# The mixer of a hybrid encoder gets a block and an instruction planner of its own

## The chip, the core and the metric

The kernel runs on one core of one Trainium2 chip. The core has five engines that each work through their own list of instructions in order: TensorE (PE, with its weight loads shown apart as PEld), VectorE (DVE), ScalarE (ACT), GpSimd (POOL) and SyncE (SP), which here issues all DMA transfers. They wait for one another through semaphores. The metric is the device time of one execution in microseconds (us).

## The reference

One layer of an encoder for 2048 tokens of width 1024, in float32. A mixer first, whose input projection feeds two recurrences: an mLSTM with 4 heads of 128, chunked, and an RWKV-7 recurrence with 8 heads of 64, in which each token changes a 64 x 64 state per head. Then attention to a memory of 256 tokens, then a gated feed-forward net with a causal convolution, each with a residual and an RMS norm:

```python
x = x + hybrid_token_mixer(rmsnorm(x, norm_mix), ...)       # mLSTM and RWKV-7 side by side
x = x + mem_cross_attn(rmsnorm(x, norm_x), rmsnorm(mem, norm_mem), x_wq, x_wkv, x_wo)
x = x + conv_glu_ffn(rmsnorm(x, norm_ffn), f_up, f_conv_w, f_conv_b, f_down)
return rmsnorm(x, norm_final)
```

and inside the mixer, for the RWKV-7 half, token by token:

```python
sk = einsum('bhvk,bhk->bhv', state, kk_t)
state = state * w_t - sk[..., None] * (kk_t * a_t) + v_t[..., None] * k_t
y = einsum('bhvk,bhk->bhv', state, r_t)
```

## The kernel before

Matrix products of weights and activations are done in two parts: a weight tile of 512 KB is loaded (`load_raw`, line 96), rounded by ScalarE into `whi` (line 101), and the rest is taken by GpSimd or VectorE into `wlo` (line 105); three products hi x hi, hi x lo, lo x hi follow. Two raw tiles and four split pairs are kept.

The first part, `mixer()`, goes over four blocks of 512 tokens. `norm_block` makes the normalised block `hA` (eight tiles, hi and lo); the dense products `pd<-hA` (31 weight tiles for each block, line 122 by the helper `mm`) feed seven streams. `rwkv_pre` prepares a head pair (16 groups in all: 4 blocks by 4 pairs), `rwkv_solve` inverts the small triangular matrices on VectorE with several round trips through DRAM, `rwkv_merge` puts them together, and `rwkv_seq` runs the recurrence over 8 chunks of each group, 128 steps in all. One step is a chain over three engines: PE makes `qy` from the state `sbd`, ACT copies `q`, PE makes `pu`, DVE copies it to `UV` (line 755), PE makes `pS` from `UV`, DVE updates `sbd` (line 761). `rwkv_tail` normalises the result. `st_ml` does the mLSTM in the same manner, and `gates` makes the gates of each block (with the transposes `gtr`). At the end of `mixer()`, `kv_prep` folds the keys and values of the memory with the query and output weights into `qk_dram` and `vo_dram`; its 32 weight tiles use the same two raw tiles, and its `mem` tiles the eight slots of `hA`.

The function `run_streams` sets the program order of all this: it calls the streams' generators one piece at a time, on a clock that counts estimated PE time alone, with waits such as `yield LU` (178 ns between `pu` and `pS`) or `LSOLVE` (39163 ns from a group's `rwkv_pre` to its merge).

Program order is not yet the engines' order. The framework plans each block of a program before it is compiled: it steps through a simulated execution, and each engine takes, among the instructions whose inputs and buffers are ready at that simulated moment, the one that stands first in program order. That fixes every engine's list, SyncE's DMA issues among them. Which instructions count as ready hangs on the durations that the planner assumes. There are two planners: the ordinary one, and one that uses a full timeline simulation of engines and queues. A block opened with `tc.block` is planned by itself, and no instruction of it is mixed with those outside. In the kernel before, the constants at the top and the whole of `mixer()` stand in the program's outer block and are planned by the ordinary one; the second part (output projection, attention, feed-forward) has been opened as

```python
ctx.enter_context(tc.block(name="attn_ffn", schedule_with_timeline_sim=True))
```

Of the kernel before, what the change touches and what calls it, by code (L numbers as in the profile page):

```python
# [56 lines left out]
def tile_hybrid_encoder(ctx: ExitStack, tc: tile.TileContext, t_in: dict, out: bass.AP, stage: str = "all"):  # L57
# [1055 lines left out]
        kv_prep(kt, sm, T, PQ, PD)  # L1113
        mx.close()

    mixer()
    wld[0] = 0
    if stage == "mix":
        nc.sync.dma_start(out, y_dram.rearrange("k p t -> (k p) t"))
# [361 lines left out]
```

## Time and profile before

| | us |
|---|---|
| median of 3 runs | 3570.65 |
| lowest and highest | 3564.45, 3571.49 |
| the profiled execution's own time | 3564.44 |
| its span, first to last instruction | 3562.6 |
| mixer, by the windows of the trace | 0 to 1515 |
| second part | 1515 to 3562 |

The profiled execution is one of the quicker ones: 6.2 us under the median. A busy time is the time in which an engine works on an instruction; a wait row says for which instruction of which engine an idle engine waited.

### The profile page before, as it was taken

To read this page: it belongs to the slowest core of one execution; us is meant where nothing else is said; L and a number is where in the kernel's file an instruction comes from. 1 tells how busy PE (TensorE), PEld (TensorE's weight loads), DVE (VectorE), ACT (ScalarE), POOL (GpSimd) and SP (SyncE) were. 2 spreads that over 40 slices of the span, in tenths; PEclk is the share of its full clock that TensorE was granted. 3 is DMA by queue.
4 is the path that set the end of the run, shared out by engine and by line. 5 is a ranking of instruction groups with operands and counts; after the bars stand their busy time and mean duration, and the time that the engine had idled before them with its cause. 6 is when DMAs were issued, how large, how long until landed. Compare 5 with 4: busy or idle time off the path is not lost.

```text
span 3562.6 us, 48272 instructions
## 1 busy us (share of the span) xinstructions
PE 3377.6 (95%) x17836; PEld 2750.2 (77%) x17836; DVE 2020.6 (57%) x4038; ACT 1256.2 (35%) x2397; POOL 1368.7 (38%) x1364
## 2 busy tenths in 40 slices
PE   7999999999989999789999999999999999999997
PEld 5777777777767778668888888888788888888886
DVE  6788888878888887433333343444453344344345
ACT  5345434544454444433222212212442222222213
POOL 5233333433333322353144434434632343443433
PEclk9999999999999999899999999999999999999998
DMA  4223222322222234685621111112566411111111
GB/s 131 80 67 111 77 72 75 111 70 68 90 73 69 73 94 146 212 269 177 222 71 43 59 42 54 54 36 71 154 219 212 141 55 36 54 54 42 54 48 54
DMA packets 203388, 342.01 MB, mean 96 GB/s; under 512 B 77072, under 2 KB 108944, under 8 KB 203152
## 3 DMA queue, kind: packets, MB, share of 16 engines
q1 hardware_dynamic: 203152, 338.92, 30.2%
q8 instruction: 141, 2.31, 0.3%
q14 instruction: 95, 0.78, 0.1%
HBM read 293.68 MB, written 45.15 MB: 95 GB/s over the span
## 4 chain that ended last, share of the span: by engine, by line
PE 55%; DMA 4%; DVE 2%; ACT 1%; issue 0%; POOL 0%; SPq 0%; DVEq 0%; ACTq 0%; POOLq 0%
PE pd L148 11%; PE pd L151 11%; PE pd L150 11%; PE dps L1354 4%; PE dps L1352 4%; PE dps L1353 4%; DMA x<-xT 2%; PE sc L1233 1%; PE sc L1235 1%; PE sc L1234 1%; DVE x L1369 0%; DMA wqk<-qk_dram 0%; PE ppt L1258 0%; DVE x L1201 0%; DMA y<-y_dram 0%
## 5 line engine op out<-in xcount | busy, mean ns | idle before, releaser
L105 POOL TENSOR_TENSOR wlo<-wraw,whi 128x512 fp32r<-128x512 f32 (+1 forms) x544 | 785.7, 1451 | 813.0 <-ACT whi L101 736.3
L122 PE MATMUL pd<-hA,whi 128*128 128x512 f32 x1984 | 677.6, 415 | 11.2 <-ACT uconv L824 5.8
L101 ACT CAST whi<-wraw 128x512 fp32r<-128x512 f32 (+1 forms) x596 | 383.4, 651 | 540.9 <-PE pd L150 222.0
L151 PE MATMUL pd<-h,wlo 128*128 128x512 f32 x1408 | 547.9, 389 | 0.0
L148 PE MATMUL pd<-h,whi 128*128 128x512 f32 x1408 | 547.9, 389 | 0.0
L150 PE MATMUL pd<-h,whi 128*128 128x512 f32 x1408 | 547.7, 389 | 0.0
L122 PEld LDWEIGHTS pd<-hA,whi 128*128 128x128 f32 x1984 | 357.5, 191 | 80.4 <-ACT hA L363 8.3
L122 PE MATMUL pd<-hA,wlo 128*128 128x512 f32 x992 | 402.2, 405 | 0.0
L1355 DVE TENSOR_TENSOR x<-dps,x 128x512 f32<-128x512 f32 x352 | 235.5, 689 | 224.3 <-PE dps L1354 222.2
L150 PEld LDWEIGHTS pd<-h,whi 128*128 128x128 f32 x1408 | 264.3, 188 | 54.8
L151 PEld LDWEIGHTS pd<-h,wlo 128*128 128x128 f32 x1408 | 264.3, 188 | 54.8
L148 PEld LDWEIGHTS pd<-h,whi 128*128 128x128 f32 x1408 | 264.3, 188 | 54.7
L1354 PE MATMUL dps<-act,wlo 128*128 128x512 f32 x704 | 271.5, 390 | 0.0
L1353 PE MATMUL dps<-act,whi 128*128 128x512 f32 x704 | 271.4, 390 | 0.0
L1352 PE MATMUL dps<-act,whi 128*128 128x512 f32 x704 | 261.6, 390 | 3.2 <-DVE x L1355 2.6
L122 PEld LDWEIGHTS pd<-hA,wlo 128*128 128x128 f32 x992 | 189.8, 191 | 34.2 <-issue 0.7
L1336 DVE SCALAR_TENSOR_TENSOR fu<-fu,pd 128x512 f32<-128x512 f32 x88 | 60.5, 688 | 226.6 <-PE pd L151 221.7
L1155 POOL TENSOR_TENSOR sq<-sq 128x512 f32<-128x512 f32 x56 | 73.9, 1320 | 252.9 <-ACT sq L1152 231.5
L1352 PEld LDWEIGHTS dps<-act,whi 128*128 128x128 f32 x704 | 132.6, 188 | 31.9 <-DVE x L1355 3.4
L1354 PEld LDWEIGHTS dps<-act,wlo 128*128 128x128 f32 x704 | 132.6, 188 | 27.6
L1353 PEld LDWEIGHTS dps<-act,whi 128*128 128x128 f32 x704 | 132.4, 188 | 27.5
L1330 POOL TENSOR_TENSOR fu<-fu,bcs 128x512 f32<-128x512 f32 x88 | 114.2, 1298 | 97.1 <-DVE fu L1329 95.6
(913 smaller groups left out, 6220.2 us busy)
## 6 DMA issues: line engine op xcount, KB each, us to landing
wraw<-w_in SPq DMA_DIRECT2D x124, 512.0 KB, 3.5
wraw<-f_up SPq DMA_DIRECT2D x88, 512.0 KB, 3.4
wqk<-qk_dram SPq DMA_DIRECT2D x64, 512.0 KB, 5.3
wvo<-vo_dram SPq DMA_DIRECT2D x64, 512.0 KB, 4.2
wraw<-f_down SPq DMA_DIRECT2D x44, 512.0 KB, 3.4
wraw<-w_out SPq DMA_DIRECT2D x32, 512.0 KB, 5.6
y<-y_dram SPq DMA_DIRECT2D x32, 256.0 KB, 7.0
x<-xT SPq DMA_DIRECT2D x32, 256.0 KB, 5.1
```

Source lines behind the costliest of these rows:

```text
L101: nc.scalar.copy(hi, raw)
L105: (nc.vector if dve else nc.gpsimd).tensor_tensor(lo, raw, hi.bitcast(F32), ALU.subtract)
L122: nc.tensor.matmul(out_, lhsT, rhs, **kw)
L148: nc.tensor.matmul(ps, hi[:, k % 4, :], a[:, 0, :n], start=(k == 0), stop=False)
L150: nc.tensor.matmul(ps, hi[:, k % 4, :], a[:, 1, :n], start=False, stop=False)
L151: nc.tensor.matmul(ps, lo[:, k % 4, :], a[:, 0, :n], start=False, stop=(k == last and not late))
L1155: (nc.vector if fast else nc.gpsimd).tensor_tensor(acc, acc, sq, ALU.add)
L1330: nc.gpsimd.tensor_tensor(u, u, bc3[b], ALU.mult)
L1352: nc.tensor.matmul(ps, hi[:, d, :], a[:, 0, :], start=(g == 0), stop=False)
L1353: nc.tensor.matmul(ps, hi[:, d, :], a[:, 1, :], start=False, stop=False)
L1354: nc.tensor.matmul(ps, lo[:, d, :], a[:, 0, :], start=False, stop=(g == GRP - 1))
L1355: nc.vector.tensor_tensor(xs[b][d], ps, xs[b][d], ALU.add)
```

## The change

```diff
@@ -1113,7 +1113,8 @@
         kv_prep(kt, sm, T, PQ, PD)
         mx.close()
 
-    mixer()
+    with tc.block(name="mixer", schedule_with_timeline_sim=True):
+        mixer()
     wld[0] = 0
     if stage == "mix":
         nc.sync.dma_start(out, y_dram.rearrange("k p t -> (k p) t"))
```

The call of `mixer()` is enclosed in a block of its own, which is planned on the full timeline simulation. The few constants made before it (`ident`, `vec`, `ones`, `nhalf`, `align`) stay in the outer block. No instruction of the computation is added, removed or changed in size; program order, tiles and buffers are the same.

## Rows read from the trace of the kernel before

**Rows 1.** Part 1 of the page: the span, then busy time by engine.

```profile
span 3562.6 us, 48272 instructions
PE 3377.6 (95%) x17836; PEld 2750.2 (77%) x17836; DVE 2020.6 (57%) x4038; ACT 1256.2 (35%) x2397; POOL 1368.7 (38%) x1364
```

**Rows 2.** Windows by stage: start:end, length, busy us (instructions) of each engine, granted clock.

```profile
core 0: us, PE busy (x) PEld busy (x) DVE busy (x) ACT busy (x) POOL busy (x), PEclk, DMA share, GB/s
0.00:100.00 100.00, 73.61 (x323) 58.26 (x323) 62.49 (x121) 58.18 (x107) 55.57 (x106) 0.97 0.40 132
100.00:1340.00 1240.00, 1151.29 (x7561) 906.57 (x7561) 1018.60 (x2547) 558.64 (x1180) 418.55 (x482) 0.98 0.27 80
1340.00:1431.00 91.00, 80.21 (x646) 71.18 (x646) 64.29 (x161) 43.15 (x106) 28.35 (x25) 0.92 0.49 152
1431.00:1515.00 84.00, 66.77 (x381) 57.42 (x379) 37.67 (x49) 34.63 (x64) 24.88 (x19) 0.88 0.70 219
1515.00:3562.00 2047.00, 2005.75 (x8928) 1656.74 (x8928) 837.52 (x1164) 561.64 (x940) 841.37 (x732) 0.99 0.30 96
```

**Rows 3.** Waits of PE up to 1515 us: total us, times, longest.

```profile
PE pS L122 <- DVE UV L755: 41.1, 43, 2.7
PE gtr L126 <- ACT xs L515: 15.0, 4, 5.3
PE ssa L322 <- DVE sq L319: 14.4, 1, 14.4
PE qy L122 <- DVE sbd L761: 12.2, 20, 2.0
```

**Rows 4.** Tile hA, the dense products: duration ns min/median/max, first and last start.

```profile
L122 PE MATMUL pd<-hA,wlo x992: 387/393/776, 21.9 to 1318.6; 128*128 128x512 f32 x199
```

**Rows 5.** Tile UV: the copy on VectorE.

```profile
L755 DVE COPY UV<-pu x128: 247/283/285, 183.7 to 1420.1; 64x128 f32<-64x128 f32 x128
```

**Rows 6.** Tile sbd: the state update on VectorE.

```profile
L761 DVE SCALAR_TENSOR_TENSOR sbd<-pS,pcol,sp x256: 240/284/293, 185.2 to 1421.8; 64x64 f32<-64x64 f32 x128
```

**Rows 7.** Tile KR: a product with two operands in SBUF.

```profile
L613 DVE TENSOR_TENSOR KR<-xs,Pt x32: 406/414/1516, 74.8 to 1310.1; 128x256 f32<-128x256 f32 x32
```

**Rows 8.** Line 105, the splits of weights, 0 to 1340 us.

```profile
L105 POOL TENSOR_TENSOR wlo<-wraw,whi x230: 1262/1291/2562, 5.5 to 1317.8; 128x512 fp32r<-128x512 f32 x115
```

**Rows 9.** Timeline around one step of the recurrence: start us, length us.

```profile
1298.91 1.53 POOL L105 TENSOR_TENSOR wlo<-wraw,whi 128x512 fp32r<-128x512 f32 x1 [1.91 <-ACT whi L101]
1299.21 1.51 DVE L613 TENSOR_TENSOR KR<-xs,Pt 128x256 f32<-128x256 f32 x1
1299.38 0.40 PE L122 MATMUL pu<-q,dg 128*66 128x64 f32 x4
...
1300.75 0.28 DVE L755 COPY UV<-pu 64x128 f32<-64x128 f32 x1
...
1301.09 0.49 PE L122 MATMUL pS<-UV,E 128*128 128x128 f32 x2 [0.56 <-DVE UV L755]
```

**Rows 10.** Windows around two waits of PE, columns as in Rows 2.

```profile
255.00:268.00 13.00, 10.34 (x63) 8.02 (x61) 12.02 (x40) 3.35 (x9) 4.29 (x6) 1.00 0.22 65
1018.00:1030.00 12.00, 9.67 (x59) 8.45 (x60) 7.78 (x23) 4.69 (x11) 1.76 (x3) 0.59 0.24 76
```

**Rows 11.** Waits of SyncE's queue up to 1515 us.

```profile
SPq L96 <- POOL wlo L105: 183.0, 34, 14.8
```

**Rows 12.** Timeline at the start of the program.

```profile
0.81 0.39 SPq L70 DMA_DIRECT2D vec<-vec  x1
0.94 0.06 DVE L78 MEMSET align<- 128x1 f32 x1
```

**Rows 13.** Timeline at the present border between mixer and second part.

```profile
1514.92 0.06 DVE L78 MEMSET align<- 128x1 f32 x1
1515.47 0.83 SPq L96 DMA_DIRECT2D wraw<-w_out  x1
...
1522.95 0.79 PE L148 MATMUL pd<-y,whi 128*128 128x512 f32 x1 [9.33 <-ACT y L1184]
```

## Prediction

> **What bounds the kernel now.** I read the page's first part, then windows cut where the work changes, then PE's waits, then the tiles of the recurrence. The span is 3562.6 us and PE is busy for 3377.6 us of it [rows 1]. The windows show two unlike halves [rows 2]. From 1515 us on PE works for 2005.8 of 2047 us at a granted clock of 0.99: the second part, which the change leaves alone. In the mixer PE is busy for 1151 of 1240 us between 100 and 1340 us and VectorE for 1019 of them (82%), so two engines are nearly full there and the lists of both matter. In the last 175 us, to 1515, PE leaves 28 us empty and the clock falls to 0.92 and 0.88.
>
> What PE waits for is a list of short waits, not one long one [rows 3]: 41.1 us in 43 waits for the copy to `UV`, 12.2 us in 20 for the state `sbd`, 15.0 us in four for the gates, and 14.4 us before its first product. A wait for `UV` or `sbd` is one of an order: PE's list has `pS` or `qy` at its head while dense products stand behind it, and the timeline shows one. `pu` starts at 1299.38, the copy at 1300.75 and `pS` at 1301.09, because VectorE was busy with the product of line 613 from 1299.21 on for 1.51 us [rows 9]. The copy itself never takes over 0.285 us and the state update never over 0.293 [rows 5, 6]: what is late is the place in VectorE's list.
>
> **The change, part by part.**
>
> *The new border.* The block ends the free mixing of the constants with the mixer. At the present border PE stands idle for 9.33 us, but that is a reload: the first weight tile is issued at 1515.47, and PE starts at 1522.95 [rows 13]. VectorE's first instruction behind it, a memset of 0.06 us, runs at 1514.92, half a us before that load is issued [rows 13], so the border itself is no long meeting of all engines. At the new one nothing stands before it but the load of `vec`, issued at 0.81 us, and memsets that end by 1 us [rows 12]. Bounds: 0, if engines pass it one by one, and 9.3, the whole hole of the other border. I take 1.5 us, near the lower end, since the mixer's first load can start some 1 us later at most.
>
> *The work.* Nothing is removed, added or resized: the 7561 matmuls and 2547 VectorE instructions of the middle window [rows 2], and every DMA, are issued again. All five lists are drawn up afresh, and SyncE's with them.
>
> *The stalls of the recurrence.* This is the term that decides. There are 128 steps, each with one copy to `UV`. 43 of them hold PE up now, a third, at 41.1/43 = 0.96 us each [rows 3]. Below: a planner whose durations match the chip would see `UV` late and put dense products before `pS`; none is hit, a gain of 41.1 us. Above: with no foresight at all a copy finds VectorE busy in 82% of cases [rows 2], 105 of 128 steps, and 105 x 0.96 = 101 us, a loss of 60 us. Which end is nearer? Whether a step is hit hangs on what VectorE does in that microsecond, and the same instruction there takes 0.41 us mostly and 1.52 at worst [rows 7]: in the timeline, 1.51 us while a GpSimd split of 1.53 us ran beside it [rows 9]. A plan fixes one duration for each instruction and one place for each split; on the chip the lists drift against each other for 1500 us, so a truer mean does not say which step is met. Against that, dense products are there to be put between. I take half of the steps: 64 x 0.96 = 61.4, so 20.3 us more than now. The `sbd` waits, 20 at 0.61 us, I leave where they are; the same scaling would add 52 us at the upper end (105 x 0.61 less 12.2).
>
> [...]
>
> *The tail.* Dense products end at 1318.6 us [rows 4]; the recurrence makes its last state update at 1421.8 [rows 6], and `kv_prep` goes on alone to 1515. The `mem` tiles sit in slots of `hA`, so `kv_prep`'s products can't be pulled before that moment by any plan. If dense work ends earlier the tail starts earlier; if the recurrence falls behind, it sticks out longer, with `kv_prep` to fill it. PE has 28 us empty there [rows 2]; a plan could gain or lose that much, and I take zero.
>
> *The second part* starts from the same DRAM tensors and its own plan: zero, give or take its first 9.3 us.
>
> Sum against the profiled execution: 3564.44 + 1.5 + 20.3 = 3586.2 us. The median shown lies 6.2 us above that execution, so 3592.4 us for a median. A change under 0.2% (7.1 us) can't be told from none in this kernel.
>
> **The rivals.**
>
> *Faster: the stalls go.* In the old planner's own picture PE cannot stand idle before `pS` with a ready dense product behind; on the chip it does so 43 times, so that picture has VectorE too quick. The full timeline may have it right. Then up to 41.1 + 12.2 = 53.3 us go, and with them lowered clock: in the stretch around the longest wait for the gates, 5.3 us, the granted clock is 0.59, though around the longest wait for `UV`, 2.7 us, it is 1.00 [rows 3, 10], so short waits cost little of it. The shortfall from 1.00 over the mixer's windows is 3 + 25 + 7 + 10 = 45 us [rows 2]. Half of the stalls and a quarter of the shortfall: 26.7 + 11.3 - 1.5 = 36.5 us gained, 3534 us. All of both would give 3474. Against it: the UV wait above, which no mean duration foretells. It decides from the point where fewer than 43 steps are hit.
>
> *Much slower: SyncE's queue.* All transfers stand in one list. Its issues of weight loads wait 34 times for a GpSimd split that frees a raw tile, 183 us together, 5.4 us each and 14.8 at most [rows 11]; behind them stand the small transfers of `rwkv_solve`. Today no wait of PE in the mixer is for a DMA among its largest [rows 3]. If the new list puts one such wait in front of each group's round trip and merges stand too early in PE's list, 16 x 5.4 = 86 us are added: 3658 us. For it: the order of program has only an estimate of the solve's length in it. It decides when the merge's first transposes wait for their load.
>
> *No change.* The two planners agree on nearly all of the order, or the block is planned as before, and the border's 1.5 us is all: 3572 us.
>
> **How the numbers follow.** More hits, as summed: 0.45. SyncE's queue: 0.09. No change: 0.10. Faster: 0.36. The first two are slower, 0.54 together. The likeliest case gives 3592 us; its own range runs from 3578, just beyond what can be told, to 3640 (3570.65 + 60 + 9.3), the two upper bounds together. The range given must hold both signs: its low end is 3512, 22 us below the faster case, and its high end 3650, short of the queue's case. I leave about 0.09 on each side.
>
> **What would show it.** Right: PE's wait for `UV` above 60 us in the mixer's window, with the number of waits nearer to 64 than 43, PE's busy time there about the same, and the dense products ending some 20 us later than 1318.6. For the faster rival: that wait well below 41 us, a clock nearer 1.00 to 1340 us, and the second part starting near 1480. For the queue: waits of PE on `dg` loads, and long SyncE waits ahead of the round trips. If all lists stand as before, the trace repeats the old waits one by one. The forecast is wrong if the new planner knows VectorE's delays well enough to fill the steps; and it is wrong in its place, not its sign, if the loss sits in the tail after the last dense product instead of in the steps.

## The result and the profile after

The change makes the kernel slower: 3768.96 us median of four runs (3761.37 to 3773.94) against 3567.55, a ratio of 1.0562 with a 95% interval of [1.054, 1.0585], 201 us. The forecast was 3592.4, at most 3650: the sign is right, the size is not. The profiled execution took 3761.37 us. Two executions marked as slow are left out of all numbers below, one of x18's four at 12290.68 us and one of the kernel before at 3788.9 us.

Part 1 of the page after, to be held against [rows 1]:

```profile
span 3759.6 us, 48403 instructions
PE 3513.0 (93%) x17836; PEld 2904.9 (77%) x17836; DVE 1971.9 (52%) x4038; ACT 1262.7 (34%) x2397; POOL 1367.3 (36%) x1364
```

The same 17836 products keep PE busy for 3513.0 us, 135 us more than before; VectorE's 4038 instructions take 49 us less. Windows by stage (start:end, length, then each engine's busy us and instructions; then the granted clock, the mean share of TensorE's full clock in that window), cut as in [rows 2] at the last dense product, the last state update and the border:

```profile
0.00:100.00 100.00, 79.29 (x367) 64.11 (x368) 67.02 (x131) 61.83 (x113) 56.94 (x110) 1.00 0.41 133
100.00:1470.00 1370.00, 1225.27 (x7057) 1006.55 (x7056) 905.04 (x2341) 533.89 (x1104) 407.17 (x463) 0.85 0.23 69
1470.00:1709.00 239.00, 203.93 (x1484) 179.04 (x1483) 161.73 (x397) 103.83 (x240) 60.12 (x57) 0.84 0.52 157
1709.00:1717.00 8.00, 2.16 (x6) 0.71 (x4) 2.03 (x5) 1.41 (x2) 3.00 (x3) 0.50 0.01 3
1717.00:3759.60 2042.60, 2002.31 (x8928) 1654.53 (x8928) 836.07 (x1166) 561.74 (x940) 840.07 (x733) 0.99 0.30 96
```

The second part is untouched (2042.6 us, clock 0.99); the mixer grows from 1515 to 1717 us. PE's busy time in it is 79.29 + 1225.27 + 203.93 + 2.16 = 1510.7 us, before it was 73.61 + 1151.29 + 80.21 + 66.77 = 1371.9 [rows 2]: 139 us of the 202 are PE working longer on the same products, at a clock of 0.85 in place of 0.98 in the long middle window, and 63 us are PE standing empty. The first 100 us are better than before (PE 79.3 against 73.6).

Where the work ends, from the tiles hA and sbd (duration ns min/median/max, first and last start), against [rows 4, 6]:

```profile
L122 PE MATMUL pd<-hA,wlo x992: 387/389/628, 24.3 to 1469.4; 128*128 128x512 f32 x199
L761 DVE SCALAR_TENSOR_TENSOR sbd<-pS,pcol,sp x256: 243/290/324, 193.7 to 1707.4; 64x64 f32<-64x64 f32 x128
```

The last dense product comes 151 us later, the last state update 286. The recurrence trailed the dense products by 103 us at the end; now it trails by 238, and ends together with `kv_prep`. PE's waits in the mixer (total us, times, longest), against [rows 3]:

```profile
PE pS L122 <- DVE UV L755: 42.4, 35, 7.0
PE qy L122 <- DVE sbd L761: 29.6, 11, 7.3
PE ssa L322 <- DVE sq L319: 14.7, 1, 14.7
PE qy L122 <- ACT yt L768: 12.7, 17, 2.1
```

The wait that the forecast built on, `UV`, has hardly moved in sum (41.1 before) and strikes fewer steps, 35 for 43. The other direction has moved. VectorE's waits before the change, mixer:

```profile
DVE UV L755 <- PE pu L122: 35.2, 36, 2.3
...
DVE sbd L761 <- PE pS L122: 16.3, 24, 1.2
```

and after it:

```profile
DVE UV L755 <- PE pu L122: 100.4, 60, 9.0
DVE sbd L761 <- PE pS L122: 74.3, 66, 4.4
DVE pr L676 <- DMA l<-rd: 57.9, 15, 7.0
```

Now VectorE stands with the recurrence's instruction at its head and waits for PE's products, 174.7 us in place of 51.5. PE is late with the recurrence. In VectorE's longest wait for `pu`, 9.0 us, PE works through 35 dense products (start:end, length, PE busy us on them, their number, granted clock):

```profile
984.80:993.80 9.00, 8.04 (x35) 1.00 0.31 110
```

Over all these waits together PE is busy for 171 of the 174.7 us, 85 of them on dense products; before it was 25 of 51.5. How the dense products lie is seen in windows of 10 us that count the dense products alone (start:end, length, PE busy us on them, their number, granted clock). After:

```profile
530.00:540.00 10.00, 0.00 (x0) 0.53 0.41 112
540.00:550.00 10.00, 0.00 (x0) 0.50 0.01 3
550.00:560.00 10.00, 7.96 (x25) 0.78 0.04 4
560.00:570.00 10.00, 8.91 (x39) 1.00 0.25 75
570.00:580.00 10.00, 8.59 (x36) 1.00 0.25 85
580.00:590.00 10.00, 0.00 (x0) 0.93 0.24 79
590.00:600.00 10.00, 0.00 (x0) 0.50 0.22 63
600.00:610.00 10.00, 3.97 (x11) 0.55 0.06 17
610.00:620.00 10.00, 9.45 (x38) 1.00 0.26 86
```

and before:

```profile
530.00:540.00 10.00, 7.49 (x28) 1.00 0.31 82
540.00:550.00 10.00, 6.50 (x24) 1.00 0.20 51
550.00:560.00 10.00, 9.53 (x41) 1.00 0.20 64
560.00:570.00 10.00, 2.64 (x11) 0.86 0.47 159
570.00:580.00 10.00, 0.71 (x2) 0.97 0.05 6
580.00:590.00 10.00, 7.42 (x27) 1.00 0.18 48
590.00:600.00 10.00, 6.54 (x23) 1.00 0.18 58
```

Before, five of these seven windows hold 23 to 41 dense products, with the recurrence's small ones between. After, they come in solid bunches, and then there are none for 20 us, in which the clock falls to 0.50. Of the 120 such windows from 100 to 1300 us, 32 hold 34 dense products or more after the change, and 14 before; 28 hold three or fewer, at a mean clock of 0.59, and 3 before. I call a window with three or fewer bare; the table below counts them for each run. The groups of PE's lines (count, busy us, mean ns, idle before) show on whom the low clock falls. Before:

```profile
L122 PE MATMUL pd<-hA,wlo 128*128 128x512 f32 x992 | 402.2, 405 | 0.0
L122 PE MATMUL qy<-UV,F 128*66 128x64 f32 (+1 forms) x1024 | 124.6, 245 | 0.0
L122 PE MATMUL pab<-KR,E 64*128 64x128 f32 x512 | 62.9, 298 | 0.8 <-DVE bv L598 0.4 <-ACT UV L622 0.3
```

and after:

```profile
L122 PE MATMUL pd<-hA,wlo 128*128 128x512 f32 x992 | 403.1, 406 | 0.0
L122 PE MATMUL qy<-UV,F 128*66 128x64 f32 (+1 forms) x1024 | 149.9, 280 | 0.0
L122 PE MATMUL pab<-KR,E 64*128 64x128 f32 x512 | 91.4, 339 | 10.2 <-DVE bv L598 6.1 <-DVE F L636 3.3 <-DVE E L611 0.8
```

A dense product costs what it did (406 ns for 405); the small ones of the recurrence (`qy`) and of its preparation (`pab`) grow by 14% in their mean. So the dense work runs ahead, at a mean clock of 0.998 in the 32 windows with 34 dense products or more, then stops for a while, and the recurrence is left to stretches of its own, at 0.59 in the 28 bare windows.

### The profile page after: what moved, and what is told of

Read it like the earlier page. It is cut to its first block, busy times and chain, and to the rows that moved or that the text cites. A ratio compares the mean times of both kernels' runs of the same rounds, so it can differ in the third digit from the quotient of the medians.

```text
span 3759.6 us, 48403 instructions
## 1 busy us (share of the span) xinstructions
PE 3513.0 (93%) x17836; PEld 2904.9 (77%) x17836; DVE 1971.9 (52%) x4038; ACT 1262.7 (34%) x2397; POOL 1367.3 (36%) x1364
## 4 chain that ended last, share of the span: by engine, by line
PE 75%; DVE 13%; DMA 6%; ACT 2%; issue 2%; SPq 1%; POOL 1%; DVEq 0%; ACTq 0%; POOLq 0%
PE pd L151 11%; PE pd L148 11%; PE pd L150 11%; PE pd L122 10%; PE dps L1355 4%; PE dps L1353 4%; PE dps L1354 4%; PE qy L122 2%; PE pab L122 2%; DVE pr L656 2%; DVE pr L676 2%; PE sc L1234 1%; PE sc L1236 1%; PE sc L1235 1%; PE p L122 1%
## 5 line engine op out<-in xcount | busy, mean ns | idle before, releaser
L122 PE MATMUL pd<-hA,whi 128*128 128x512 f32 x1984 | 662.8, 411 | 24.0 <-DVE xs L482 8.6
L122 PEld LDWEIGHTS pd<-hA,whi 128*128 128x128 f32 x1984 | 377.6, 195 | 108.0 <-ACT hA L363 13.0
L122 PE MATMUL qy<-UV,F 128*66 128x64 f32 (+1 forms) x1024 | 149.9, 280 | 0.0
```

Source lines behind the costliest of these rows:

```text
L122: nc.tensor.matmul(out_, lhsT, rhs, **kw)
```

## The experiments

Each was timed beside the kernel before on the same chip; none leaves out work, and x7 and x8 add useless products. The columns: ratio to before with its 95% interval; start of the last dense product and of the last state update; PE's wait for `UV` (us, times); VectorE's waits for `pu` and `pS` together; bare windows of 120; granted clock over the span. Where the list of an engine is held, the planner draws up the other engines' lists anew around it; they are not those of the change or of the kernel before.

| run | median us | ratio | last dense | last `sbd` | `UV` wait | VectorE waits | bare | clock |
|---|---|---|---|---|---|---|---|---|
| before | 3567.55 | 1 | 1318.6 | 1421.8 | 41.1, 43 | 51.5 | 3 | 0.981 |
| the change | 3768.96 | 1.0562 [1.054, 1.0585] | 1469.4 | 1707.4 | 42.4, 35 | 174.7 | 28 | 0.930 |
| x1_border | 3570.66 | 1.0013 [1.0001, 1.0025] | 1323.1 | 1425.2 | 40.4, 43 | 51.7 | 5 | 0.981 |
| x2_pe_tl | 3774.25 | 1.0582 [1.0558, 1.0605] | 1530.1 | 1715.7 | 60.6, 46 | 123.5 | 18 | 0.946 |
| x3_pe_ord | 3854.20 | 1.0804 [1.0779, 1.083] | 1603.3 | 1719.9 | 94.8, 41 | 120.8 | 21 | 0.939 |
| x4_lead40 | 3660.15 | 1.0255 [1.0229, 1.0281] | 1437.7 | 1604.1 | 19.6, 24 | 130.9 | 10 | 0.957 |
| x17_lead120 | 3650.69 | 1.0229 [1.021, 1.0248] | 1417.0 | 1591.4 | 18.8, 26 | 145.3 | 9 | 0.964 |
| x5_tl_oldpe | 3656.91 | 1.0241 [1.0217, 1.0266] | 1413.0 | 1518.7 | 50.2, 35 | 84.9 | 5 | 0.967 |
| x6_ord_newpe | 3898.91 | 1.0912 [1.0884, 1.0939] | 1581.0 | 1840.3 | 21.9, 32 | 222.1 | 32 | 0.911 |
| x9_tl_oldpe_dve | 3583.12 | 1.0041 [1.0025, 1.0058] | 1341.6 | 1448.3 | 32.8, 33 | 78.5 | 3 | 0.978 |
| x10_tl_oldpe_sp | 3662.18 | 1.0265 [1.0236, 1.0294] | 1407.8 | 1514.8 | 51.3, 34 | 73.8 | 6 | 0.967 |
| x11_tl_oldpe_act | 3636.52 | 1.0188 [1.0158, 1.0217] | 1395.6 | 1501.6 | 63.6, 45 | 63.1 | 4 | 0.969 |
| x12_tl_olddve | 3963.43 | 1.1110 [1.1079, 1.114] | 1690.7 | 1836.6 | 49.2, 73 | 407.4 | 16 | 0.921 |
| x7_fill3 | 3790.55 | 1.0615 [1.058, 1.065] | 1480.1 | 1726.8 | 18.5, 12 | 192.8 | 28 | 0.941 |
| x8_fill3_old | 3697.88 | 1.0358 [1.0328, 1.0388] | 1432.0 | 1546.9 | 53.0, 25 | 105.2 | 4 | 0.974 |
| x14_dve10 | 3860.66 | 1.0822 [1.0796, 1.0848] | 1548.3 | 1672.3 | 43.2, 66 | 312.5 | 16 | 0.921 |
| x15_lead40_dve10 | 3801.56 | 1.0656 [1.0633, 1.068] | 1502.9 | 1617.2 | 33.6, 30 | 270.1 | 11 | 0.939 |
| x16_lead40_dve10_act10 | 3779.31 | 1.0584 [1.0563, 1.0605] | 1482.3 | 1586.5 | 27.1, 36 | 207.8 | 17 | 0.944 |
| x18_lead120_dve50 | 3674.33 | 1.0294 [1.0258, 1.033] | 1407.4 | 1550.0 | 31.4, 30 | 157.4 | 8 | 0.957 |
| x19_dve50 | 3738.95 | 1.0468 [1.0431, 1.0505] | 1439.6 | 1612.8 | 27.3, 40 | 126.6 | 25 | 0.939 |

**The border or the planner?** The block without the timeline simulation, shown against the changed kernel:

```diff
-    with tc.block(name="mixer", schedule_with_timeline_sim=True):
+    with tc.block(name="mixer"):
```

> The mixer in a block of its own, but planned by the ordinary planner. Theory 'lead' (the full-timeline plan puts dense products far ahead of the recurrence on PE's list, and the recurrence is then left alone at a lowered clock): the time of the kernel before, 3567 us give or take 7, since the plan is the old one and the border costs at most 2 us. Theory 'other lists' (VectorE, ScalarE or SyncE got bad lists, PE's follows): the same. Theory 'border' (the block itself makes the engines meet, or keeps work from being mixed over its edge): 3700 us or more, most of the 201 us.

The border costs 1.3 per mille, 4.6 us with an interval of 0.4 to 8.9. All the rest of the 201 us is the planner.

**PE's list in program order.** Every product and transpose of the mixer but `kv_prep`'s is chained to the one before it, under the new planner (x2) and under the ordinary one (x3):

```diff
-        nc.tensor.matmul(out_, lhsT, rhs, **kw)
+        pinned(nc.tensor.matmul(out_, lhsT, rhs, **kw).ins)
```

> The changed kernel, with PE's list of the mixer's streams held to program order by order-only edges from each matmul or transpose to the one before it (kv_prep's left free); all other lists are still drawn up by the full-timeline planner. Theory 'lead': the loss goes, 3540 to 3620 us; dense products end around 1320 to 1360 us, the recurrence within some 110 us of them, and the granted clock of the mixer is 0.95 or more. Theory 'other lists': 3700 us or more, PE waits longer for VectorE or for DMA.

> The kernel before (ordinary planner, no block) with the same edges: PE's list of the streams is program order. Both theories: near the kernel before, 3560 to 3620 us. It says what the ordinary planner's own moves on PE's list are worth, and with the run of the changed kernel under the same edges it compares the two planners on all the other lists alone: 'lead' has the two within 30 us, 'other lists' has this one faster by 100 us or more.

Program order is no remedy: both are far slower than before, and the ordinary planner alone loses 8%. 'Lead' expected at most 3620 us for both and failed; x3, expected within 30 us of x2 or 100 faster, is 80 slower. What the ordinary planner moves on PE is worth 288 us (3854.2 against 3565.9 for the kernel before, timed beside it). The `UV` wait is 94.8 us there, by far the largest: with no freedom on PE the stall of the forecast does appear.

**How far the dense products may run ahead.** Under the new planner, a dense product may not be queued before the last product of another kind that stands `LEAD` or more places earlier in PE's program order, 40 in x4 and 120 in x17. It is one edge for each dense product; other products further back are held by it only indirectly:

```diff
+            if dense:
+                i = len(peq) - LEAD
+                while i > 0 and not peq[i - 1][1]:
+                    i -= 1
+                if i > 0:
+                    tc.add_manual_dep(ins, peq[i - 1][0].name, ...)
```

> The changed kernel with one rule for dense products alone: such a product may not be queued before any other PE instruction that stands 40 or more places before it in program order. All else is free. Theory 'lead': 3540 to 3640 us, the stretches without dense products shrink and the clock of the mixer is back to 0.95 or more. Theory 'other lists': 3700 us or more.

> PE's bound alone, at 120 places in place of 40. Theory 'lead': between 3660 (40 places) and 3769 (none), near 3710. Rival 'finer order': the size of the bound tells nothing; as likely below 3660 or near 3769.

Either bound wins back 109 to 118 of the 201 us, with the recurrence done 103 and 116 us sooner and 9 or 10 bare windows in place of 28. PE's busy time in the mixer falls with it, from 1510.7 to 1419.5 us in x17. x4 lies just beyond the range that 'lead' gave it (3540 to 3640). PE's waits of x17:

```profile
PE qy L137 <- DVE sbd L780: 20.2, 18, 3.0
PE pS L137 <- DVE UV L774: 18.8, 26, 3.3
```

Both waits together, 39.0 us, are shorter than the 53.3 of the kernel before [rows 3], and yet the run is 81 us slower than the kernel before: the waits of PE for the recurrence are not what sets the time. The expectation for x17, a time between 40 places and none, missed: 120 is no worse than 40. What a bound can win back sits in leads beyond 120 places.

**Which list carries it.** The new planner with single engines held to the order that the kernel before has on them, and the reverse (x6: the ordinary planner with PE's list of after):

```diff
+    for eng, packed in ORDER.items():
+        ...
+        for a, b in zip(order, order[1:]):
+            tc.add_manual_dep(made[b], made[a].name, ...)
```

> The changed kernel with PE's list of the whole mixer held to the list that the kernel before has, by order-only edges; the four other lists are drawn up by the full-timeline planner around it. Theory 'PE's list' (the whole loss sits in the order of PE's instructions; the other engines follow): 3540 to 3590 us. Theory 'other lists': 3650 us or more.

> The reverse: no block, the ordinary planner for four lists, PE's list held to that of the changed kernel. Theory 'PE's list': 3730 to 3800 us, as slow as the changed kernel. Theory 'other lists': under 3620 us.

PE's list is worth 112 us beside the new planner's other lists (3769 to 3657), the same as a bound on its lead gave. But 87 us stay with PE's old list, and PE's new list beside the ordinary planner's others is worse than all of the new and outside both ranges expected: a list does not keep its worth beside others.

> With PE's list of before held, the new planner's other four lists still cost 86 us. This holds VectorE's list of before as well; ScalarE, GpSimd and SyncE stay as newly planned. Theory 'VectorE carries it' (the copies to UV and the updates of sbd stand behind other work in the new list): under 3590 us, PE's UV wait back near 41 us. Rival 'SyncE' (small transfers of the solve behind weight loads): 3640 to 3660. Theory 'lists belong together': a held list beside three new ones costs, so no gain or a loss, 3640 to 3700.

> PE's and SyncE's lists of before held, VectorE, ScalarE and GpSimd as newly planned. Rival 'SyncE': under 3600 us, dense products end near 1330 us. Theory 'VectorE carries it': 3640 to 3670, no change from 3657.

> PE's, ScalarE's and GpSimd's lists of before held, VectorE and SyncE as newly planned. Theories 'VectorE' and 'SyncE' both: 3640 to 3670, no change from 3657. If the weights' rounding and splitting come late in the new lists of ScalarE and GpSimd: under 3600 us.

> VectorE's list of before held alone, the other four, PE's among them, as newly planned. Theory 'PE's list costs 112 us because it runs ahead of the recurrence': still above 3730 us even if VectorE's part is undone, since PE's dense products stay ahead. Theory 'lists belong together': above 3769, as the new PE list beside the ordinary planner's other lists gave 3899. If VectorE's list carries all of it: under 3640.

With VectorE's old list too, the time is within 0.41% of before: VectorE's list carries 74 us of what x5 left (3656.9 to 3583.1). The windows of x9, 300 us each, show the mixer of before again, PE busy for 93% at a clock of 0.97:

```profile
700.00:1000.00 300.00, 279.14 (x1823) 220.33 (x1821) 236.15 (x615) 128.43 (x284) 96.09 (x116) 0.97 0.25 76
```

SyncE's list is worth nothing (3662 against 3657), ScalarE's and GpSimd's 20 us. And VectorE's old list alone, beside a list of PE that the new planner draws around it, is the slowest run of all, where VectorE waits longest for PE's products:

```profile
DVE UV L775 <- PE pu L142: 289.9, 74, 8.9
DVE sbd L781 <- PE pS L142: 117.5, 60, 6.1
```

VectorE has the recurrence as early as the kernel before, PE has it late, and VectorE's list stands still until PE comes. This run has 16 bare windows, fewer than the change: their number alone doesn't give the time.

**Is it the clock?** Three useless products of 384 columns behind `pu` in each of the 128 steps, with PE's list held (x7), and the same in the kernel before as a control (x8):

```diff
+                for _ in range(NFILL):
+                    fillers.append((nc.tensor.matmul(qyf[:, P:TB], blkr, whh[:, 0:TB - P], ...).ins, anchor.ins.name))
```

> The changed kernel with PE's list held as it is, and three useless products of 384 columns (never read) added behind pu in each of the 128 steps, while PE would wait for UV: about 0.16 us each at the full clock, 61 us of added work if nothing hides them. Theory 'clock' (the lowered clock in stretches without dense products is itself a cause of the loss): the granted clock of the mixer rises and the time falls, to 3640 to 3740 us, in spite of the work. Theory 'clock is a sign only': the time rises to between 3769 and 3830 us.

> The control: the same three useless products a step in the kernel before, its PE list held. The clock is 0.98 there already. Both theories: the time rises by 10 to 61 us, to 3576 to 3630 us, which is what the products cost where they have no clock to win.

The fillers cost 128 us in the kernel before and 22 us after the change, where the clock over the span rises from 0.930 to 0.941. So about 106 us of the filling is free there. Part of it fills PE's empty time, which the run can't separate from what a higher clock gives back. The control also missed its expectation, at most 61 us; the fillers of x7, then of x8:

```profile
L786 PE MATMUL qy<-whh,blkr 128*128 128x384 f32 x384 | 116.5, 418 | 0.0
L786 PE MATMUL qy<-whh,blkr 128*128 128x384 f32 x384 | 101.7, 374 | 0.0
```

They occupy PE for 101.7 us in the control, 0.26 us each. The 0.16 of the expectation is what line 121 of the kernel reckons for 384 columns (`n_ / 2.4`), an estimate that no run shows. No run holds PE's new list without fillers, so what the holding costs is not known. Inconclusive for the share of the clock; no filling makes the change faster.

The trace of the change itself says more. The same product of the recurrence from 540 to 550 us, at a granted clock of 0.50, and from 560 to 570 us, at 1.00:

```profile
L122 PE MATMUL qy<-UV,F 128*128 128x64 f32 x4 | 1.0, 394 | 0.0
L122 PE MATMUL qy<-UV,F 128*128 128x64 f32 x4 | 0.6, 262 | 0.0
```

Added up one by one (they overlap, so the sums exceed the busy time), PE's 8908 products of the mixer last 2802 us before and 2975 after. With each put at the mean of its form at the full clock, the sums are 2732 and 2735 us, the same. So products last longer after the change because more of them run at the lower clock, 0.50: of the 5932 that are not dense, 313 ran wholly there before and 2027 after.

**A bound on VectorE as on PE.** No instruction of VectorE may be queued before a copy to `UV` or an update of `sbd` that stands 10 or more places earlier: alone (x14), with PE's bound of 40 (x15), with the like on ScalarE (x16). Then the bound of 50 places for VectorE's work on the dense side alone, with PE's bound of 120 (x18) and without (x19):

```diff
+            if k >= 0 and mine[k]:
+                last = made[k]
+            if last is not None and not mine[r]:
+                tc.add_manual_dep(ins, last.name, ...)
```

> The full timeline planner; on VectorE no instruction may be queued before a copy to UV or an update of sbd that stands 10 or more places earlier in VectorE's program order. PE is free. Theory 'lead': the recurrence is no longer held up on VectorE, so its products are ready earlier and PE's list follows: well under 3769 us, 3650 to 3720. Rival 'finer order': no gain, 3740 to 3800, or a loss as with the held list of VectorE (3963).

> The bound of 40 places on PE's dense products and that of 10 places on VectorE, both. Theory 'lead': the two engines' shares add up, 3570 to 3610 us, dense products end near 1340 us, the recurrence about 100 us later. Rival 'finer order': about 3660, as with PE's bound alone, or slower.

> As the run before, and on ScalarE no instruction may be queued before a copy of q or of yt that stands 10 or more places earlier. ScalarE's list cost about 20 us of the 86 (3657 against 3636.5 with ScalarE's and GpSimd's lists of before): theory 'lead' says up to 20 us faster than the run before; rival: within 10 us of it.

> PE's bound at 120 places, and on VectorE only the work that serves the dense products (the outputs uconv, pm, xs, qc, og, wlo, sq) may not be queued before a copy to UV or an update of sbd 50 or more places earlier; the solve, the merge and the mLSTM stay free. Theory 'the lead of the dense side, on both engines': 3570 to 3620 us. Rival 'order among the rest': within 20 us of 3651.

> The same bound of 50 places on VectorE's dense side, PE free. Theory 'the lead of the dense side': since PE's dense products need VectorE's evictions, their lead shrinks too, 3650 to 3740 us. Rival 'order among the rest': 3750 to 3800.

My theory that a lead on VectorE costs as it does on PE falls: x14, x15 and x18 all lie above the ranges that it gave. The tight bound adds 92 us to the change and 141 to x4, and VectorE then waits for `pu` and `pS` for 312.5 and 270.1 us: it forces VectorE to stand before PE is there, as x12 did. ScalarE's bound gives 22 us back. The looser bound on the dense side wins 30 us alone, at the far end of what was expected, and beside PE's bound it loses 24.

## Why the prediction was wrong

*The stalls of the recurrence: the step that failed.* The forecast called this "the term that decides", took half of the 128 steps for hit and added 20.3 us. Measured: 35 steps hit, 1.21 us each, 1.3 us more than before. The `sbd` waits, left where they were, added 17.4. Together 18.7 us of 202. That the sign came out right is luck: the term that carried it measured 1.3 us. Even the upper bounds, 60 and 52 us, would not have held the loss, since the term has the wrong place in it: it takes VectorE for late and PE for waiting. After the change PE is late with the recurrence and VectorE waits (174.7 us for 51.5).

*"PE's busy time there about the same"* was false, and it is the larger share: 139 us of the 202. It comes with the lower clock, 0.50, at which the mixer spent 96 us before and 497 after. The forecast used lowered clock only as a gain of the faster rival (45 us of shortfall that could go) and never as a loss that a bunched list could make. The sum had no term for it.

*The tail, taken as zero*, named the right event: the recurrence did fall behind and stick out. The second part's first product after, from the timeline (start us, length us, then the wait before it):

```profile
1725.00 0.79 PE L148 MATMUL pd<-y,whi 128*128 128x512 f32 x1 [10.25 <-DMA y<-y_dram]
```

From the last dense product to it, it is now 1725.0 - 1469.4 = 255.6 us; before, 1522.9 - 1318.6 = 204.3 [rows 4, 13]: 51 us more. The other 151 us are lost before the last dense product, so the loss isn't mainly in the tail either.

*Why the list is so.* Shown: bounding the lead of the dense products, or holding PE's old list, wins back 109 to 118 us, and with PE's and VectorE's old lists held together all but about 14 us are gone (3583.1 against 3568.7 for the kernel before, timed beside it). Argued only: that the timeline planner takes the chain's instructions for ready later than the ordinary one does and fills the time with dense products until their buffers are full. No run opens the planner. The forecast doubted the planner's durations, but saw only more short waits come of it.

*The border*, 1.5 us, was right within its interval. *The first loads* were better than taken: PE gained 5.7 us in the first 100. *The second part* as predicted.

*SyncE's queue*, the slower rival: the waits of weight loads for a split did grow from 183.0 us [rows 11] to 297.2, and VectorE waits 57.9 us for a round trip's load, but that load's wait falls to 13.6 and 6.1 us when PE's lead is bounded (x4, x17), SyncE's old list gains nothing beside PE's (x10), and no wait of PE for a load is among its four largest. *Faster* is refuted: the old planner's order, with its 43 short waits, is the better one. *No change* is what x1 is.

*What stays open:* what in VectorE's new list costs the 74 us beside PE's old one, and how much of the 139 us is not the clock but a chain alone overlapping less. Five kernels aimed at the first showed only that it is not a lead over the recurrence that a bound of 10 or 50 places cures. A hint, not a proof: VectorE waits 21.4 us for the round trip's load in x5, 19.4 in x10 and 0.2 in x9, where it has its old list. No version faster than the kernel before was found; the planner's better start, 5.7 us, is too little to tell.

## What to carry to other kernels

Ask of a new order not only which short waits it adds, but how far one kind of work can run ahead of another and what PE has left to do when it stops: count the large products in small windows, since here the recurrence left alone on PE paid twice, in waits (VectorE's for its products, 174.7 us for 51.5) and in clock (0.59 in the bare windows). Wait sums can fall while the time grows (x17: 39.0 us for 53.3, and 81 us slower); look at who waits for whom, in both directions, and at busy time for the same count of instructions. Lists of several engines are one plan: putting one engine's list of one plan beside the other plan's lists was worse than either plan in two cases of three (x6, x12; x5 lies between).

## What the hardware showed

The granted clock stayed at 0.50 while PE was busy without a gap. All products of PE, after the change (columns as in the windows by stage):

```profile
520.00:530.00 10.00, 8.46 (x43) 6.71 (x42) 4.21 (x9) 2.12 (x4) 3.27 (x3) 1.00 0.24 61
530.00:540.00 10.00, 5.80 (x35) 4.99 (x35) 6.16 (x16) 2.78 (x9) 0.57 (x2) 0.53 0.41 112
540.00:550.00 10.00, 10.00 (x58) 9.16 (x57) 4.88 (x15) 2.31 (x5) 0.19 (x1) 0.50 0.01 3
560.00:570.00 10.00, 10.00 (x55) 8.45 (x54) 4.52 (x9) 4.32 (x9) 4.10 (x3) 1.00 0.25 75
```

From 530 to 540 us PE has 4.20 us of gaps and the clock is 0.53, after 1.00 in the window before. In the next window PE is busy for all of 10.00 us (as the profile models the ends of products) with 58 small products, none of them dense, and the clock stays at 0.50; from 560 us on, with 39 dense products among 55, it is 1.00. That the lower clock outlasts the gap, under a PE that is busy for a whole window, is what the row of 540 us shows; what lowers the clock and what raises it again, no run shows.
